# A forget gate's power by halves of the tokens, weight splits tied behind its series, and bias tiles by pair of heads, in a fused two-layer decoder kernel

## The chip, the cores and the metric

The kernel runs on one core of a Trainium2 chip. The metric is device time in microseconds (us) of one execution, and the median over several runs is compared. The engines are named as in the profile: PE is TensorE (matmuls and transposes), DVE is VectorE, ACT is ScalarE, POOL is GpSimd, and SP is SyncE, whose queue issues nearly all DMAs. Each engine works through its own queue of instructions in order and waits there for what an instruction needs.

## The reference

Two decoder layers work on 256 tokens of width 1024 in float32: a mixture of dilated sliding-window attentions with a SwiGLU feed-forward, then "forgetting attention" with another feed-forward. The change lies in the forgetting attention:

```
proj = h @ w_in
q, k, v = qkv[:, :, 0], qkv[:, :, 1], qkv[:, :, 2]
log_f = log_sigmoid(proj[..., 3 * ATTN_WIDTH:] + b_f)        # 16 heads, 256 tokens
c = cumsum(log_f, axis=1)
s = (q @ k^T) * scale + c[query] - c[key]                    # causal
o = softmax(s) @ v
```

The term c[query] is the same for a whole row of the softmax, so that only a bias by key, taken from c, has to be added to the scores before the mask and the softmax.

## The kernel before, in words

Matrix products are computed at nearly float32 accuracy from two halves. A weight piece of 128x2048 floats is loaded as two `raw` tiles of 128x1024 (SP, L89, five buffers). ACT casts each to `wh` (L74) and DVE writes the rest to `wl` = raw - wh (L76); `wh` and `wl` have four buffers each, one for each piece. `mm3` (L188) then makes three matmuls of each product: high by high, high by low, low by high. `weights` (L142) hands out a piece, and issues the load, the cast and the split of all pieces up to AHEAD = 2 further along a fixed order. In the forgetting layer this order is GATED (the values of heads 8 to 11 with the 16 gate columns), two pieces of values, and then, by quarter of the heads, (0,0), (0,1), (1,0), (1,1), (2,0), (2,1), (3,0), (3,1), (3,2): in (quarter, w), w = 0 is q, 1 is k and 2 is v. A quarter is four heads, and two pairs `pr` of heads.

The stage runs so. PE projects GATED for the first 128 tokens (t = 0), then the other two pieces of values for them, then the same for t = 1. After each GATED projection DVE adds the bias `bf` to the gate columns (L867) and so fills half of tile `gates` (128 tokens by 2 x 16). The second `norm_t` (L173) runs in the middle of the t = 0 values: DVE scales `xn` in two halves (L179) and PE transposes them (L184). After the second GATED projection `log1p` (L776) works on both halves at once, 128x32: two DVE instructions, a power e^t on POOL (L780), and 14 more DVE instructions, a series for log(1 + e^t). It has high priority in the scheduler, which decides the order on each engine when the kernel is built.

Then PE goes through the units: (0,0), (0,1), (1,0) and so on, each 48 matmuls of 256 columns, in two halves c of 24. `gates_2` (L791) is due after the first half of unit (0,0): two transposes of the gates on PE (L795), a cumulative sum on DVE (the scan of L799), and two DMAs that write it to tile `sums` in HBM (L801). `bias(hq)` (L803) reads the sums of four heads back, broadcast to all 128 partitions (L806, 128x1536, two buffers), and adds the causal mask to two blocks of each head on POOL (L808, 128x1024). It is due after unit (0,0) for quarters 0 and 1, and later for quarters 2 and 3.

`scores_b(hq, pr)` (L814) lets PE compute the scores of a pair into two PSUM banks `sc` (L822); DVE adds the bias (L828), which frees the bank, takes the row maximum (L832), ACT takes the exponential (L277), and DVE and ACT scale by the reciprocal sum (L839, L838). For quarter 0 the first pair's scores stand after the first half of unit (1,0) and the second pair's after its second half. Both use the same two `sc` banks: the second waits until the first pair's two bias adds have read them.

Of the kernel before, what the change touches and what calls it, by code (L numbers as in the profile page):

```python
# [10 lines left out]
F32 = mybir.dt.float32  # L11
F32R = mybir.dt.float32r
AF = mybir.ActivationFunctionType
ALU = mybir.AluOpType
AX = mybir.AxisListType

P = 128
# [3 lines left out]
NH = 16  # L21
# [10 lines left out]
def trunk(ctx: ExitStack, tc: tile.TileContext, T, out):  # L32
    nc = tc.nc
# [3 lines left out]
    ap = ctx.enter_context(tc.tile_pool(name="ap", bufs=1))  # L37
# [5 lines left out]
    def first():  # L43

        return tc.high_priority(offset=300)

    def psum(tag):
        return ps.tile([P, 512], F32, tag=tag, name=f"ps_{tag}", bufs=2)
# [10 lines left out]
    def const(name, shape):  # L59
        c = cst.tile(shape, F32, name=name)  # L60
        nc.sync.dma_start(c, T[name])
        return c
# [5 lines left out]
    euler = cst.tile([P, 1], F32, name="euler")  # L68
# [60 lines left out]
    order = [("a_in", hq * 9 + g * 3 + w) for hq, g, w in a_units]  # L129
# [8 lines left out]
    AHEAD = 2  # L138
    ready = {}
    state = {"next": 0}  # L140

    def weights(nm, i, after=None):  # L142

        upto = order.index((nm, i)) + AHEAD
        while state["next"] <= min(upto, len(order) - 1):
            key = order[state["next"]]
            cuts = []
            ready[key] = piece(key, cuts)
            for cut in cuts:
                cut(after)  # L150
            state["next"] += 1
        return ready.pop((nm, i))
# [147 lines left out]
    def stat_tile(tag, n):  # L300
        return ap.tile([P, n], F32, tag=tag, name=tag, bufs=3)
# [14 lines left out]
    for i, c in enumerate(room):  # L316
        b = 1 + (i > 1)
        n = S + 512
# [31 lines left out]
    sums = ap.tile([P, D], F32, tag="xn", name="sums", bufs=2)  # L350
# [3 lines left out]
    def square(i):  # L354
        return nc.scalar.activation(part[i].rearrange("p (j s) -> p j s", s=S), xs[i], AF.Square, scale=D ** -0.5)
# [5 lines left out]
    for k in range(KT):  # L361
        if k % 4 == 0:
            w = tuple(wp.tile([P, 2048], F32R, tag=y, name=y, bufs=4) for y in ("wh", "wl"))
        g, u = g_a[:, k:k + 1], slice(k % 4 * 512, k % 4 * 512 + 512)
        with first(), in_order(cut):
            if k == 0:
                a = nc.vector.tensor_scalar(hi[:, k], xk[k], g, None, op0=ALU.mult)
            else:
                a = nc.scalar.activation(hi[:, k], xk[k], AF.Copy, scale=g)
            b = nc.vector.scalar_tensor_tensor(lo[:, k], xk[k], g, hi[:, k].bitcast(F32), op0=ALU.mult,  # L370
                                               op1=ALU.subtract)
            with in_order((a, b)):
                cut = split(w, lambda y: y[:, u], wk[k])
        if k in (1, 5, 7):
            with first(), in_order(cut):
                a = [square(i) for i in {1: (0, 1), 5: (2,), 7: (3,)}[k]][-1]
# [12 lines left out]
    with first(), in_order(cut):  # L389
        a = square(4)  # L390
# [130 lines left out]
    def later(i, fn, *a):  # L521
        due.setdefault(i, []).append((fn, a))

    quads = [{"hq": hq, "fm": {}, "pt": {}, "v": {}} for hq in range(4)]
    for i, (hq, g, w) in enumerate(a_units):
        quad = quads[hq]
        if i == 3:
            o = o_next
        elif i:

            wt = weights("a_in", hq * 9 + g * 3 + w, read if i > 4 else None)
# [9 lines left out]
        if i in (24, 31):  # L541
            x.append(hrow("x"))
            t = len(x) - 1
            nc.sync.dma_start(x[t], T["x"][t * P:(t + 1) * P, :])
        if w < 2:
# [4 lines left out]
            if i == 2:  # L550
                values_12(quad["v"], lead)

                wt = weights("a_in", 1)
# [13 lines left out]
            if w == 1:  # L567

                j = i + (hq == 0)
# [5 lines left out]
                if g == 2:  # L575
                    later(j + 1, softmax_a, quad)
                    j = 9 * hq + 11 + 2 * (hq == 0)
# [8 lines left out]
        elif i > 1:  # L586


            half = hq % 2 if g == 0 else g - 1
# [164 lines left out]
    causal = const("causal", [P, P])  # L754
# [17 lines left out]
    ga = ap.tile([P, 6, 2 * NH], F32, tag="gates", name="gates", bufs=1)  # L772
    sums = dr.tile([NH, 3 * P], F32, name="sums")
    own = (slice(0, 64), slice(64, 128))

    def log1p():  # L776
        zt, m, t, s, w, a = (ga[:, i, :] for i in range(6))
        nc.vector.tensor_scalar(m, zt, -1.0, 0.0, op0=ALU.mult, op1=ALU.max)
        nc.vector.scalar_tensor_tensor(t, m, -2.0, zt, op0=ALU.mult, op1=ALU.subtract)
        nc.gpsimd.tensor_tensor(t, euler.to_broadcast([P, 2 * NH]), t, op=ALU.pow)  # L780
        nc.vector.tensor_scalar(s, t, 0.5, 1.0, op0=ALU.mult, op1=ALU.add)
        nc.vector.reciprocal(s, s)
        nc.vector.tensor_tensor(s, s, t, op=ALU.mult)
        nc.vector.scalar_tensor_tensor(w, s, 0.25, s, op0=ALU.mult, op1=ALU.mult)
        nc.vector.tensor_scalar(a, w, 1.0 / 17, None, op0=ALU.mult)
        for n in (15, 13, 11, 9, 7, 5, 3):
            nc.vector.scalar_tensor_tensor(a, a, 1.0 / n, w, op0=ALU.add, op1=ALU.mult)
        nc.vector.scalar_tensor_tensor(a, a, 1.0, s, op0=ALU.add, op1=ALU.mult)
        nc.vector.tensor_tensor(m, m, a, op=ALU.add)

    def gates_2():  # L791

# [7 lines left out]
        for y, n in ((0, P), (P, S)):  # L800
            nc.sync.dma_start(sums[:, y:y + n], cs[:, :n])  # L801

    def bias(hq):  # L803

        b = ap.tile([P, 12 * P], F32, tag="bias", name="bias", bufs=2)
        nc.sync.dma_start(b, sums[hq * 4:hq * 4 + 4].rearrange("h c -> (h c)").partition_broadcast(P))  # L806
        d = b.rearrange("p (h b j) -> p h b j", h=4, b=3)[:, :, 0:3:2]
        nc.gpsimd.tensor_tensor(d, d, causal[:, None, None, :].to_broadcast([P, 4, 2, P]), op=ALU.add)  # L808
        bq[hq]["bias"] = b

    ot = fm_tile("ot", KT, 1)
    bq = {hq: {} for hq in range(4)}

    def scores_b(hq, pr):  # L814
        b = bq[hq]
        nm = stat_tile("nm_b", 4)
        den = stat_tile("den_b", 4)
        pt = b.setdefault("pt", {})
        scs = [psum("sc") for _ in range(2)]
        for qb in range(2):  # L820
            for h in range(2):
                last = nc.tensor.matmul(scs[h][:, qb * P:qb * P + (qb + 1) * P], b[0][own[h], pr, qb * P:(qb + 1) * P],  # L822
                                        b[1][own[h], pr, :(qb + 1) * P], start=True, stop=True)
        for h in range(2):
            s = p_tile()
            with first():
                n = (pr * 2 + h) * 3 * P
                nc.vector.tensor_tensor(s[:, :3 * P], scs[h][:, :3 * P], b["bias"][:, n:n + 3 * P], op=ALU.add)  # L828
            for qb in range(2):
                j = h * 2 + qb  # L830
                sv = s[:, qb * P:qb * P + (qb + 1) * P]
                nc.vector.tensor_reduce(nm[:, j:j + 1], sv, axis=AX.X, op=ALU.max, negate=True)  # L832
                exps(sv, nm, den, j)
            pt[pr, h] = s
        c = stat_tile("c_b", 4)
        nc.vector.reciprocal(c, den)
        for h in range(2):
            nc.scalar.activation(pt[pr, h][:, :P], pt[pr, h][:, :P], AF.Copy, scale=c[:, h * 2:h * 2 + 1])  # L838
            nc.vector.tensor_scalar(pt[pr, h][:, P:3 * P], pt[pr, h][:, P:3 * P], c[:, h * 2 + 1:h * 2 + 2], None,  # L839
                                    op0=ALU.mult)  # L840
        return last
# [12 lines left out]
        split(ot, lambda x: x[:, hq * 2 + pr, :], o[:, :S])  # L854

    wz, oz = weights(*GATED), [psum("sc") for _ in range(2)]
    ws = [weights("b_in", i * 3 + 2) for i in range(2)]
    os = [psum("mm") for _ in range(2)]
    vs = [v_tile() for _ in range(3)]

# [10 lines left out]
        bq[i][2] = vs[i]  # L871
    for t in range(2):
        proj_gated(t)
        if t == 1:
            with first():
                log1p()
        for i in range(2):
            hook = (6, lambda: norm_t(*hs[1], g_b, xt, 1)) if i > t else None
            proj_pair(xt, ws[i], os, i, (t,), hook)
        v_pair(vs[:2], os[t], t)  # L880
    later(2.5, gates_2)
    for hq in range(2):
        later(3, bias, hq)
    for i, (hq, w) in enumerate(b_units):
        if i < 3:
            continue
        wt = weights("b_in", hq * 3 + w)
        o = psum("mm")
        if w < 2:
            for c in range(2):  # L890
                proj_feat(xt, wt, o[:, c * S:(c + 1) * S], c)
                if c == 0:
                    for fn, a in due.pop(i - 0.5, ()):
                        fn(*a)
            if w == 0:

                for fn, a in due.pop(i, ()):
                    fn(*a)
            bq[hq][w] = ap.tile([P, 2, S], F32, tag=f"fm{w}", name=f"fb{w}", bufs=2)
            nc.scalar.activation(bq[hq][w], o.rearrange("p (a b) -> p a b", a=2), AF.Copy, scale=(0.125, 1.0)[w])  # L900
            if w == 1:
                j = i + 1

                for pr in range(2):
                    due.setdefault(j - 0.5 + pr / 2, []).insert(0, (scores_b, (hq, pr)))
                if hq < 2:
                    later(j + 1, bias, hq + 2)
                later(j + 1, trans_b, hq, 0)
                later(j + 1.5, pv_b, hq, 0)
                later(j + 1.5, trans_b, hq, 1)  # L910
                later(j + 2, pv_b, hq, 1)
        else:
            for t in range(2):
                proj_tok(xt, wt, o[:, t * S:(t + 1) * S], t)
                if t == 0:
                    for fn, a in due.pop(i - 0.5, ()):
                        fn(*a)
            bq[hq][w] = v_tile(o)
        for fn, a in due.pop(i, ()):
            fn(*a)  # L920
# [20 lines left out]
    for o, (a, b) in zip(acc, ((0, 512), (512, 256), (768, 256))):  # L941
        s = slice(a, a + b)
# [109 lines left out]
```

## Time and profile before

| What | Value |
|---|---|
| time, median of 3 runs | 760.62 us (759.85 to 761.73) |
| the profiled execution's own time | 759.32 us |
| its span, first to last instruction | 757.5 us |
| PE busy | 743.0 us (98%) |
| DVE, ACT, POOL busy | 500.8, 374.8, 60.5 us |
| mean granted TensorE clock | 0.994 |
| moved by DMA | 138.08 MB, mean 182 GB/s |

The profile is of one execution. A timeline row gives the start in us, the duration, the engine, the line, the operation, output<-input, the number of instructions, and in brackets the idle time before it with what ended it; a row of several instructions gives their common stretch. A matmul's duration overlaps the next one's: what PE needs for one is read from the distance of the starts.

### The profile page before, as it was taken

What the parts mean: (1) busy time and instruction counts of PE and PEld (TensorE: products, weight loads), DVE (VectorE), ACT (ScalarE), POOL (GpSimd) and SP (SyncE); (2) the same over time, 40 slices, a digit from 0 to 9 for tenths busy, and PEclk for the clock granted to TensorE, in tenths of its full rate; (3) what the DMA queues carried; (4) which work ended last, traced back from release to release, by engine and by line L of the source; (5) the groups of instructions that cost most, each with busy time, mean ns of one, the idle gap of its engine ahead of it and who ended that gap; (6) DMA issues with size and microseconds to landing.
All of it is one profiled execution on the core that took longest, in us unless ns stands there. A gap on an engine that the chain in (4) does not pass through costs nothing.

```text
span 757.5 us, 14517 instructions
## 1 busy us (share of the span) xinstructions
PE 743.0 (98%) x6008; PEld 684.8 (90%) x6008; DVE 500.8 (66%) x756; ACT 374.8 (49%) x620; POOL 60.5 (8%) x93
## 2 busy tenths in 40 slices
PE   9999999999999999999999998899999999999996
PEld 7998989999988899999999987889889999999995
DVE  6997977876887566555555474599756655556533
ACT  7636347436346555344554444367645434455421
POOL 0600003004003000000000012221000000000000
PEclk9999999999999999999999999899999999999999
DMA  9955554553655266655667353854426665556601
GB/s 335 307 178 168 182 187 124 203 195 115 195 178 182 81 225 226 197 192 186 203 198 246 125 177 114 284 181 159 161 81 224 226 198 192 188 201 204 215 2 55
DMA packets 39010, 138.08 MB, mean 182 GB/s; under 512 B 4480, under 2 KB 5920, under 8 KB 38944
## 3 DMA queue, kind: packets, MB, share of 16 engines
q1 hardware_dynamic: 38800, 137.06, 54.4%
q8 instruction: 47, 0.77, 0.4%
q14 instruction: 19, 0.16, 0.1%
q10 hardware_dynamic: 144, 0.10, 0.0%
HBM read 136.07 MB, written 1.07 MB: 181 GB/s over the span
## 4 chain that ended last, share of the span: by engine, by line
PE 90%; issue 3%; ACT 2%; DVE 2%; DMA 2%; POOL 1%; SPq 0%; POOLq 0%; ACTq 0%; DVEq 0%
PE ps_mm L196 31%; PE ps_mm L191 16%; PE ps_tr L196 9%; PE ps_sc L196 8%; PE ps_o L196 7%; PE ps_tr L191 5%; PE ps_sc L191 4%; PE ps_o L191 3%; PE ps_o L298 2%; PE ps_tr L287 2%; ACT wh L74 1%; PE ps_sc L822 1%; PE ps_sc L444 1%; DMA otl<-in_lead 1%; PE ps_sc L460 1%
## 5 line engine op out<-in xcount | busy, mean ns | idle before, releaser
L74 ACT ACTIVATE wh<-raw 128x1024 fp32r<-128x1024 f32 x236 | 243.9, 1055 | 251.3 <-PE ps_mm L196 88.2
L76 DVE TENSOR_TENSOR wl<-raw,wh 128x1024 fp32r<-128x1024 f32 x236 | 287.7, 1238 | 90.1 <-ACT wh L74 89.9
L191 PE MATMUL ps_mm<-xt,wh 128*128 128x256 f32 x816 | 228.9, 281 | 0.5 <-DVE qk L428 0.5
L196 PE MATMUL ps_mm<-xt,wl 128*128 128x256 f32 x816 | 227.2, 279 | 0.1
L196 PE MATMUL ps_mm<-xt,wh 128*128 128x256 f32 x816 | 226.9, 278 | 0.0
L191 PEld LDWEIGHTS ps_mm<-xt,wh 128*128 128x128 f32 x816 | 154.6, 190 | 4.2 <-issue 3.3
L196 PEld LDWEIGHTS ps_mm<-xt,wl 128*128 128x128 f32 x816 | 154.5, 189 | 0.4 <-DVE wl L76 0.3
L196 PEld LDWEIGHTS ps_mm<-xt,wh 128*128 128x128 f32 x816 | 154.5, 189 | 0.0
L196 PE MATMUL ps_tr<-xt,wh 128*128 128x256 f32 x304 | 83.8, 276 | 0.0
L196 PE MATMUL ps_tr<-xt,wl 128*128 128x256 f32 x304 | 83.8, 276 | 0.0
L191 PE MATMUL ps_tr<-xt,wh 128*128 128x256 f32 x304 | 83.6, 276 | 0.0
L687 DVE TENSOR_TENSOR sa<-ps_tr,sa 128x256 f32<-128x256 f32 x38 | 16.1, 424 | 73.9 <-PE ps_tr L196 73.9
L196 PEld LDWEIGHTS ps_tr<-xt,wl 128*128 128x128 f32 x304 | 57.1, 188 | 0.0
L196 PEld LDWEIGHTS ps_tr<-xt,wh 128*128 128x128 f32 x304 | 57.0, 188 | 0.0
L191 PEld LDWEIGHTS ps_tr<-xt,wh 128*128 128x128 f32 x304 | 56.9, 188 | 0.0
L191 PE MATMUL ps_mm<-wh,xt 128*128 128x256 f32 (+1 forms) x160 | 53.0, 331 | 0.0
L196 PE MATMUL ps_mm<-wh,xt 128*128 128x256 f32 (+1 forms) x164 | 51.9, 320 | 0.0
L196 PE MATMUL ps_mm<-wl,xt 128*128 128x256 f32 (+1 forms) x164 | 51.8, 320 | 0.0
L273 POOL COPY v<-v 32x256 f32<-32x256 f32 x64 | 33.2, 519 | 179.6 <-ACT v L269 176.9
L161 POOL TENSOR_SCALAR rs<-ssq 128x1 f32<-128x1 f32 x7 | 2.2, 319 | 429.6 <-ACT junk L170 429.6
L196 PEld LDWEIGHTS ps_mm<-wl,xt 128*128 128x128 f32 x164 | 30.8, 188 | 2.5
L196 PEld LDWEIGHTS ps_mm<-wh,xt 128*128 128x128 f32 x164 | 30.5, 188 | 2.6
(218 smaller groups left out, 1136.9 us busy)
## 6 DMA issues: line engine op xcount, KB each, us to landing
raw<-in_gu SPq DMA_DIRECT2D x88, 512.0 KB, 4.4
raw<-in_a_in SPq DMA_DIRECT2D x68, 512.0 KB, 4.7
raw<-in_dn SPq DMA_DIRECT2D x44, 512.0 KB, 4.6
raw<-in_b_in SPq DMA_DIRECT2D x24, 512.0 KB, 4.6
raw<-in_a_out SPq DMA_DIRECT2D x8, 512.0 KB, 5.1
raw<-in_b_out SPq DMA_DIRECT2D x8, 512.0 KB, 4.4
bias<-sums SPq DMA_DIRECT2D x4, 768.0 KB, 5.1
grow<-in_norms SPq DMA_DIRECT2D x4, 512.0 KB, 5.8
```

The costliest lines, as they stand in the source:

```text
L74: a = nc.scalar.activation(view(hi), src, AF.Copy)
L76: return a, nc.vector.tensor_tensor(view(lo), src, view(hi).bitcast(F32), op=ALU.subtract)
L161: nc.gpsimd.tensor_scalar(m, s, rest, None, op0=ALU.add)
L191: nc.tensor.matmul(o, sh, mh, start=start, stop=False)
L196: last = nc.tensor.matmul(o[:, u], s, m[:, u], start=False, stop=end and u.stop == n)
L273: nc.gpsimd.tensor_copy(v[1 + a % 2][n:n + 32, a // 2 * S:a // 2 * S + S], by_t[a * 32:a * 32 + 32, t, g])
L287: nc.tensor.transpose(tr[:, i * P:(i + 1) * P], b, ident)
L298: nc.tensor.matmul(o[h * HD:(h + 1) * HD], v[:, c:c + HD], w(h), start=start, stop=stop)
L444: nc.tensor.matmul(scs[h][:, qb * P:qb * P + (qb + 1) * P], q[hr[h], pr, qb * P:(qb + 1) * P], k[hr[h], pr, :(qb + 1) * P], start=True, st ...
L460: nc.tensor.matmul(sc[h][c, o:o + 64], q[hr[h], pq, qb * P + a * 32:qb * P + a * 32 + 32], k[hr[h], pq].rearrange("p (b n) -> p b n", b=2) ...
L687: nc.vector.tensor_tensor(a, u, sg, op=ALU.mult)
L822: last = nc.tensor.matmul(scs[h][:, qb * P:qb * P + (qb + 1) * P], b[0][own[h], pr, qb * P:(qb + 1) * P], b[1][own[h], pr, :(qb + 1) * P], ...
```

## The change

- `power(half)` takes the two DVE instructions and POOL's power out of `log1p` and runs them on 128x16: for the tokens of t = 0 after their GATED projection, and for t = 1 after theirs, directly ahead of the rest of `log1p`, which stays on both halves.
- `weights` gets its reach as an argument. The second piece of values now reaches one piece ahead, not two, so that piece (0,1) is loaded and split with the unit (0,0), together with (1,0). These four splits on DVE are tied behind the last instruction of `log1p` (their ACT casts are not).
- `bias` works by pair of heads: DMAs of 128x768, masks of 128x512, and four buffers of half the size. Quarter 0's two are due after unit (0,0), as before, and quarter 1's two after unit (1,0).

Nothing of what is computed changes. The diff, cut to its core (`log1p`'s unchanged lines left out):

```
-    def weights(nm, i, after=None):
-        upto = order.index((nm, i)) + AHEAD
+    def weights(nm, i, after=None, ahead=AHEAD):
+        upto = order.index((nm, i)) + ahead
...
-    def log1p():
-        zt, m, t, s, w, a = (ga[:, i, :] for i in range(6))
+    def power(half):
+        zt, m, t = (ga[:, i, half * NH:(half + 1) * NH] for i in range(3))
         nc.vector.tensor_scalar(m, zt, -1.0, 0.0, op0=ALU.mult, op1=ALU.max)
         nc.vector.scalar_tensor_tensor(t, m, -2.0, zt, op0=ALU.mult, op1=ALU.subtract)
-        nc.gpsimd.tensor_tensor(t, euler.to_broadcast([P, 2 * NH]), t, op=ALU.pow)
+        nc.gpsimd.tensor_tensor(t, euler.to_broadcast([P, NH]), t, op=ALU.pow)
+
+    def log1p():
+        _, m, t, s, w, a = (ga[:, i, :] for i in range(6))
...
-        nc.vector.tensor_tensor(m, m, a, op=ALU.add)
+        return nc.vector.tensor_tensor(m, m, a, op=ALU.add)
...
-    def bias(hq):
-        b = ap.tile([P, 12 * P], F32, tag="bias", name="bias", bufs=2)
-        nc.sync.dma_start(b, sums[hq * 4:hq * 4 + 4].rearrange("h c -> (h c)").partition_broadcast(P))
-        d = b.rearrange("p (h b j) -> p h b j", h=4, b=3)[:, :, 0:3:2]
-        nc.gpsimd.tensor_tensor(d, d, causal[:, None, None, :].to_broadcast([P, 4, 2, P]), op=ALU.add)
-        bq[hq]["bias"] = b
+    def bias(hq, pr):
+        b = ap.tile([P, 6 * P], F32, tag="bias", name="bias", bufs=4)
+        nc.sync.dma_start(b, sums[hq * 4 + pr * 2:hq * 4 + pr * 2 + 2].rearrange("h c -> (h c)").partition_broadcast(P))
+        d = b.rearrange("p (h b j) -> p h b j", h=2, b=3)[:, :, 0:3:2]
+        nc.gpsimd.tensor_tensor(d, d, causal[:, None, None, :].to_broadcast([P, 2, 2, P]), op=ALU.add)
+        bq[hq]["bias", pr] = b
...
-    ws = [weights("b_in", i * 3 + 2) for i in range(2)]
+    ws = [weights("b_in", i * 3 + 2, ahead=2 - i) for i in range(2)]
...
         proj_gated(t)
-        if t == 1:
-            with first():
-                log1p()
+        with first():
+            power(t)
+            last = log1p() if t else None
...
     for hq in range(2):
-        later(3, bias, hq)
+        for pr in range(2):
+            later(3 + 2 * hq, bias, hq, pr)
...
-        wt = weights("b_in", hq * 3 + w)
+        wt = weights("b_in", hq * 3 + w, last if i == 3 else None)
```

DVE's queue from the end of the two instructions ahead of the second (before: the only) power. Before, splits of weights (L76) stand between the instructions of the series:

```order
L779 SCALAR_TENSOR_TENSOR gates<-gates 128x32
L781 TENSOR_SCALAR gates<-gates 128x32
L782 RECIPROCAL gates<-gates 128x32
L76 TENSOR_TENSOR wl<-raw,wh 128x1024
L783 TENSOR_TENSOR gates<-gates 128x32
L76 TENSOR_TENSOR wl<-raw,wh 128x1024
L784 SCALAR_TENSOR_TENSOR gates<-gates 128x32
L785 TENSOR_SCALAR gates<-gates 128x32
L76 TENSOR_TENSOR wl<-raw,wh 128x1024
L787 SCALAR_TENSOR_TENSOR gates<-gates 128x32
L76 TENSOR_TENSOR wl<-raw,wh 128x1024
L787 SCALAR_TENSOR_TENSOR gates<-gates 128x32 x5
```

The same place of the changed kernel, in whose numbering L784 to L792 are the series and L802 is the scan:

```order
L779 SCALAR_TENSOR_TENSOR gates<-gates 128x16
L784 TENSOR_SCALAR gates<-gates 128x32
L785 RECIPROCAL gates<-gates 128x32
L786 TENSOR_TENSOR gates<-gates 128x32
L787 SCALAR_TENSOR_TENSOR gates<-gates 128x32
L788 TENSOR_SCALAR gates<-gates 128x32
L790 SCALAR_TENSOR_TENSOR gates<-gates 128x32 x7
L791 SCALAR_TENSOR_TENSOR gates<-gates 128x32
L792 TENSOR_TENSOR gates<-gates 128x32
L76 TENSOR_TENSOR wl<-raw,wh 128x1024 x5
L802 SCALAR_TENSOR_TENSOR v<-v,ps_tr 16x256
L76 TENSOR_TENSOR wl<-raw,wh 128x1024 x5
```

The series now stands in one piece. Five splits have moved behind it and ahead of the scan, the sixth behind the scan.

SP's queue from the load of a norm's row (`grow`) on, while PE still projects the gates' second half; before:

```order
L56 DMA grow<-in_norms 128x1024
L89 DMA raw<-in_b_in 128x1024 x6
L801 DMA sums<-v 16x128
L801 DMA sums<-v 16x256
L89 DMA raw<-in_b_in 128x1024
L806 DMA bias<-sums 128x1536 x2
L89 DMA raw<-in_b_in 128x1024 x3
L806 DMA bias<-sums 128x1536
```

And in the changed kernel:

```order
L56 DMA grow<-in_norms 128x1024
L89 DMA raw<-in_b_in 128x1024 x4
L804 DMA sums<-v 16x128
L804 DMA sums<-v 16x256
L89 DMA raw<-in_b_in 128x1024 x2
L809 DMA bias<-sums 128x768 x4
L89 DMA raw<-in_b_in 128x1024 x2
L809 DMA bias<-sums 128x768
```

The sums are written after four loads of weights, not six, and the first read of the bias stands behind six such loads, not seven. On PE the two transposes of the gates stand behind 24 matmuls of unit (0,0), where they stood behind 38; from the first scores on, PE's order is the same.

More of the change, by code (lines that the diff above doesn't have):

```diff
@@ L826, in scores_b @@
             with first():
-                n = (pr * 2 + h) * 3 * P
-                nc.vector.tensor_tensor(s[:, :3 * P], scs[h][:, :3 * P], b["bias"][:, n:n + 3 * P], op=ALU.add)
+                bias_h = b["bias", pr][:, h * 3 * P:(h + 1) * 3 * P]
+                nc.vector.tensor_tensor(s[:, :3 * P], scs[h][:, :3 * P], bias_h, op=ALU.add)
             for qb in range(2):
@@ L906, in trunk @@
                 if hq < 2:
-                    later(j + 1, bias, hq + 2)
+                    for pr in range(2):
+                        later(j + 1, bias, hq + 2, pr)
                 later(j + 1, trans_b, hq, 0)
```

## The prediction

> **What bounds the kernel now.** I read the page first: how busy PE is says whether other engines matter at all. Its rows are the share of the span, and the granted clock in 40 slices.
>
> ```profile
> span 757.5 us, 14517 instructions
> PE 743.0 (98%) x6008; PEld 684.8 (90%) x6008; DVE 500.8 (66%) x756; ACT 374.8 (49%) x620; POOL 60.5 (8%) x93
> PEclk9999999999999999999999999899999999999999
> ```
>
> PE sets the end. A change can only gain where PE stands still or runs slowly, and the one slice with an 8 lies at 473 to 492 us. So the waits of PE come next (us in total, times, longest):
>
> ```profile
> PE ps_tr L795 <- DVE gates L789: 5.7, 1, 5.7
> PE ps_o L307 <- POOL euler L69: 0.9, 1, 0.9
> PE ps_mm L191 <- DVE qk L428: 0.5, 1, 0.5
> ```
>
> One wait is worth having: the transposes of the gates for the series. PE's timeline around it, and the windows after it (length, PE busy, clock, DMA share, GB/s):
>
> ```profile
> 466.43 0.29 PE L191 MATMUL ps_mm<-xt,wh 128*128 128x256 f32 x1
> ...
> 470.63 0.28 PE L196 MATMUL ps_mm<-xt,wh 128*128 128x256 f32 x1
> 476.61 0.60 PE L795 MATMUL ps_tr<-ident,gates 128*16 128x128 f32 x2 [5.70 <-DVE gates L789]
> 476.86 0.56 PE L196 MATMUL ps_mm<-xt,wl 128*128 128x256 f32 x1
> 477.22 0.42 PE L191 MATMUL ps_mm<-xt,wh 128*128 128x256 f32 x1
> ...
> 482.30 0.28 PE L191 MATMUL ps_mm<-xt,wh 128*128 128x256 f32 x1
> ...
> 488.65 0.28 PE L196 MATMUL ps_mm<-xt,wl 128*128 128x256 f32 x1
> 488.86 0.93 PE L822 MATMUL ps_sc<-fb,fb 64*128 64x128 f32 x8
> ...
> 492.65 1.03 PE L822 MATMUL ps_sc<-fb,fb 64*128 64x128 f32 x8
> 476.60:482.30 5.70, 5.69 (x28) 0.51 0.67 236
> 482.30:488.65 6.35, 6.35 (x58) 1.00 0.93 308
> ```
>
> From 482.30 to 488.65 there are 56 steps of 0.1134 us each. From 477.22 to 482.30 there are 24 matmuls at 0.212: after the wait PE runs for 5.7 us at clock 0.51. That is a second price of the same wait: 24 x (0.212 - 0.1134) = 2.4, and about 0.3 for the transposes and the matmul behind them. The wait costs 5.7 + 2.4 + 0.3 = 8.4 us. Another way gives the same: unit (0,0) starts at 466.43, and 120 matmuls stand before the first scores (38 ahead of the transposes, 82 behind them); 120 x 0.1134 = 13.6, with 0.4 for the transposes 480.4, against 488.86.
>
> The Trainium skill (TensorE: Matmul & The Clock Gate, Part 1) says that an idle window of about 3.4 us halves the clock and about 3.4 us of work restores it. The halving agrees; the slow stretch here was 5.7 us, so the measured price of 2.7 stands, where 3.4 us at half speed would be an estimated 1.7.
>
> Why DVE is late, from its own timeline and POOL's:
>
> ```profile
> 461.11 0.17 DVE L867 TENSOR_TENSOR gates<-ps_sc,bf 128x16 f32<-128x16 f32 x1 [2.67 <-PE ps_sc L196]
> 461.54 0.19 DVE L779 SCALAR_TENSOR_TENSOR gates<-gates 128x32 f32<-128x32 f32 x1
> 467.27 0.18 DVE L781 TENSOR_SCALAR gates<-gates 128x32 f32<-128x32 f32 x1 [5.54 <-POOL gates L780]
> 467.49 0.35 DVE L782 RECIPROCAL gates<-gates 128x32 f32<-128x32 f32 x1
> 472.76 1.09 DVE L787 SCALAR_TENSOR_TENSOR gates<-gates 128x32 f32<-128x32 f32 x5
> 475.01 1.22 DVE L76 TENSOR_TENSOR wl<-raw,wh 128x1024 fp32r<-128x1024 f32 x1
> 476.14 0.18 DVE L788 SCALAR_TENSOR_TENSOR gates<-gates 128x32 f32<-128x32 f32 x1
> 477.24 0.68 DVE L799 TENSOR_TENSOR_SCAN v<-v,ps_tr 16x256 f32<-16x256 f32 x1 [0.69 <-PE ps_tr L795]
> 452.37 1.56 POOL L164 TENSOR_TENSOR rs<-rs,mhalf 128x1 f32<-128x1 f32 x1 [0.33 <-DVE gates L867]
> 461.81 5.43 POOL L780 TENSOR_TENSOR gates<-euler,gates 128x32 f32<-128x32 f32 x1 [7.89 <-DVE gates L779]
> L164 POOL TENSOR_TENSOR rs<-rs,mhalf x7: 566/572/1557, 255.2 to 747.0; 128x1 f32<-128x1 f32 x7
> ```
>
> The power holds the series until 467.27; then six splits share DVE with it until 476.55.
>
> **The change part by part.** *Power by halves.* The 128x32 power took 5.43 us, a 128x1 power 0.57. The line through both gives 0.57 + 15 x 0.157 = 2.9 for 128x16; the ends are 2.7 (half) and 5.43 (nothing saved). I take 2.9. The first half's power starts about 454.9 and is over by 457.8, or a microsecond later if it is stretched as the power at 452.37 was beside a split; nothing on POOL stands behind it. It costs DVE two instructions of 0.2 us, one between the two halves of `xn`: the second half ends 0.2 later, hidden by PE's first four transposes; uncovered, 0.2 us. The second power starts at 461.85 as before and ends at 464.75.
>
> *The series in one piece.* 14 instructions, 13 at 0.22 (five took 1.09) and the reciprocal at 0.38: 3.2 us, from 464.8 to 468.0. PE comes to the transposes after 24 matmuls, at 466.43 + 24 x 0.1134 = 469.15. That is 1.1 us of cover: the wait of 5.7 and the slow clock go, 8.4 us. With a power of 5.43 the series would end at 470.5 and PE wait 1.4.
>
> *The splits behind it.* Each takes 1.13 (475.01 to 476.14). Unit (0,1) starts at 466.43 + 48 x 0.1134 + 0.4 = 472.3 and needs its two, done at 469.1 and 470.3; unit (1,0), at 477.7, has its own by 472.5. No wait, with 2 us of cover; uncovered, the lateness itself. ACT's casts keep their order. Its copy of unit (0,0)'s result must free a PSUM bank by 477.7; it stands behind a cast whose load is issued at 470.3 and lands, at a median of 5.2 us, at 475.5, so the copy ends at about 477.1: covered by 0.6.
>
> ```profile
> DMA to landing us min/median/max: 4.0/5.2/6.0
> 468.95 7.63 SPq L89 DMA_DIRECT2D raw<-in_b_in  x6
> 477.94 0.81 SPq L801 DMA_DIRECT2D sums<-v  x2
> 482.00 0.85 SPq L806 DMA_DIRECT2D bias<-sums  x2
> DMA to landing us min/median/max: 3.4/3.5/3.6
> DMA to landing us min/median/max: 4.1/6.0/7.5
> 488.16 5.86 POOL L808 TENSOR_TENSOR bias<-bias,causal 128x1024 f32<-128x1024 f32 x2 [20.92 <-DMA bias<-sums]
> 499.04 2.40 POOL L808 TENSOR_TENSOR bias<-bias,causal 128x1024 f32<-128x1024 f32 x1 [5.02 <-DMA bias<-sums]
> 491.70 1.01 DVE L828 TENSOR_TENSOR p<-ps_sc,bias 128x384 f32<-128x384 f32 x2
> 488.66 3.12 DVE L76 TENSOR_TENSOR wl<-raw,wh 128x1024 fp32r<-128x1024 f32 x1 [0.20 <-ACT wh L74]
> ```
>
> The three lines of landings are those of the six weight loads of 465 to 480, of the two writes of the sums, and of the first three bias reads.
>
> *The bias by pairs.* This is what can come late next. Before, the first pair's adds ended at 492.71 and PE began the second pair's scores, which overwrite their banks, at 492.65: no slack. PE now comes there 3.8 us (492.65 - 488.86) after 480.4, at 484.2. The bias: five splits (5.65) stand ahead of the scan, which ends at 468.0 + 5.65 + 0.7 = 474.4; the second write is issued at 474.8 and lands after 3.5, at 478.3. The sixth load ahead of the bias needs the sixth split, over at 475.5, and holds nothing up. So the first read goes at 478.3, 3.7 earlier than before. Its landing: the first 768 KB read took 6.0, a lone one 4.1; for 384 KB behind two weight loads I take 4.0, with 3.0 and 6.0 as ends: 482.3. The mask of half the size: half of 2.40 to half of 3.4 (488.16 to about 491.6, when the first add waited for it), 1.4 taken, 2.4 if halving saves nothing: 483.7. Two adds, 1.0: 484.7. PE waits 0.5 us. By the ends: 0, or 478.3 + 6.0 + 2.4 + 1.0 - 484.2 = 3.5.
>
> A rule that speaks against halving the reads, from the Trainium skill (DMA: Bandwidth & Descriptors, Anatomy of one DMA): about 2.0 us of each DMA is fixed, the rest goes by 436 GB/s. The lone read agrees roughly (estimate 3.8, measured 4.1); for 384 KB it gives an estimate of 2.9, and PE would not wait: 752.2.
>
> Eight masks of half the size instead of four: the POOL work is the same. While a mask ran, a split took 3.12 instead of 1.22; that happens in shorter pieces, and PE waited for none of it before. A quarter-2 read now stands in SP's queue ahead of loads for units 30 us away: nothing.
>
> **Sum.** -8.4 + 0.5 = -7.9. The profiled execution, 759.32, would take 751.4; the median, 760.62, lies 1.3 above it and becomes **752.7**. A difference under 0.3% (2.3 us) can't be told from none here.
>
> **The rivals.** *The bias later still (0.18).* Longer reads or masks, up to the ends above: PE waits 1.5 to 3.5, giving 753.7 to 755.7; if the clock falls after such a wait as it did after 5.7, another 2.7, up to 758.4. For it: adds and scores met without slack before. Against it: the reads are half as long.
>
> *The power doesn't shrink (0.06).* PE waits 1.4 at the transposes; all behind the series comes 2.55 later, so the adds end at 487.25 against 485.6: 3.1 lost, 755.3. Against: the 0.57 of one column.
>
> *The first power holds DVE (0.03).* If POOL's power comes ahead of the second half of `xn` on what they share, as the mask did to the split, that half waits up to 2.9, PE up to 2.5: 8.4 - 0.5 - 2.5 gives 755.2. Against: `xn` starts as L779 ends, the power some 0.1 later.
>
> *The wait only moves (0.04).* If reads and masks saved nothing at all, the adds would follow the scan's end by 492.71 - 477.92 = 14.8, at 489.2: a wait of 5.0 and 2.7 of slow clock against the 8.4, 759.9: no change.
>
> *Slower (0.03).* If something pins the adds to the clock time they have now (the sums' write or the reads held by the weight loads, which are all issued earlier), PE comes at 484.2 and waits until 492.7: 8.5 + 2.7 - 8.4 = 2.8 slower, 763.4. It is slower by over 0.3% only if the adds end after 492.2. Against: the only loads ahead of the reads are free by 475.5.
>
> **How the numbers follow.** The forecast has 0.66. Its wait of 0 to 1.5 gives 752.2 to 753.7; the runs shown scatter by 0.9 around their median, so I start at 751.0. Rivals two and three and most of the first lie under 756.0, which is the upper end. Faster: 0.66 + 0.18 + 0.06 + 0.03, less 0.02 for the first rival's far end: 0.91. Same: 0.04 + 0.02 = 0.06. Slower: 0.03.
>
> **What would show it.** Right: no wait of PE at the gates' transposes, clock 1.00 from 475 to 485, a power of about 2.9 us, series over at 468, first scores at about 480.4, first mask starting near 482.3. Wrong: a wait of PE at the second pair's scores of over 1.5 us, or of any length at the transposes; a power near 5 us; a slow clock after either.

## The result, and the profile after

The changed kernel took **754.2 us** in the median of five runs (753.28 to 755.8), the kernel before, on the same chip, 760.63. The ratio is 0.9915, with a 95% interval of 0.9899 to 0.9931: faster by 6.4 us, inside the range, 1.5 us above the number forecast. Below, differences of under 0.3% are again told as none, unless their interval is narrower.

The page of the changed kernel, its span, its busiest engine and the granted clock in 40 slices. The profiled execution is the slowest of the five, 755.8 us:

```profile
span 754.0 us, 14536 instructions
PE 742.7 (98%) x6008; PEld 683.7 (91%) x6008; DVE 499.1 (66%) x758; ACT 376.2 (50%) x620; POOL 61.9 (8%) x98
PEclk9999999999999999999999999999999999999999
```

The slice with an 8 is gone. The waits of PE (us in total, times, longest):

```profile
PE ps_sc L825 <- DVE p L831: 2.0, 1, 2.0
PE ps_sc L380 <- ACT wh L74: 1.0, 2, 0.8
PE ps_o L307 <- POOL euler L69: 0.9, 1, 0.9
```

The 5.7 us at the gate transposes are gone too, and the series' last instruction is in no row. A new wait stands first: the second pair's scores (L825) wait for the adds of the bias (L831). The two others lie in the first 60 us of the kernel. PE's timeline through the stage, in this execution, whose unit (0,0) begins 0.5 us later than in the one of before (466.95 against 466.43):

```profile
469.69 0.38 PE L798 MATMUL ps_tr<-ident,gates 128*16 128x128 f32 x2
481.08 0.93 PE L825 MATMUL ps_sc<-fb,fb 64*128 64x128 f32 x8
486.90 1.38 PE L825 MATMUL ps_sc<-fb,fb 64*128 64x128 f32 x8 [1.97 <-DVE p L831]
```

The transposes come without a wait, and the first scores 7.8 us earlier than at 488.86. From there to the second scores it took 3.8 us before; now it is 5.8, because of the 1.97 in brackets. The windows behind the transposes and behind that wait (length, PE busy, clock, DMA share, GB/s):

```profile
476.60:484.70 8.10, 8.10 (x71) 1.00 0.99 310
486.90:492.00 5.10, 5.10 (x27) 0.67 0.92 305
```

Where PE ran at 0.51 before, it now runs at 1.00. But behind the new wait the clock fell in this execution: 5.1 us at 0.67, that is 5.1 x (1 - 0.67) = 1.7 us lost. Next, POOL's and DVE's timelines, for the power and the series:

```profile
455.39 3.35 POOL L780 TENSOR_TENSOR gates<-euler,gates 128x16 f32<-128x16 f32 x1 [0.95 <-DVE gates L779]
462.31 2.90 POOL L780 TENSOR_TENSOR gates<-euler,gates 128x16 f32<-128x16 f32 x1 [3.57 <-DVE gates L779]
465.25 0.18 DVE L784 TENSOR_SCALAR gates<-gates 128x32 f32<-128x32 f32 x1 [3.02 <-POOL gates L780]
468.34 0.19 DVE L792 TENSOR_TENSOR gates<-gates 128x32 f32<-128x32 f32 x1
468.45 5.76 DVE L76 TENSOR_TENSOR wl<-raw,wh 128x1024 fp32r<-128x1024 f32 x5
474.13 0.67 DVE L802 TENSOR_TENSOR_SCAN v<-v,ps_tr 16x256 f32<-16x256 f32 x1
```

A power of 2.90, a series of 3.28 in one piece (465.25 to 468.53), five splits in 5.76, and the scan over at 474.80. The way from there to the adds, by SP's issues, POOL's masks and DVE's adds:

```profile
469.70 3.73 SPq L89 DMA_DIRECT2D raw<-in_b_in  x4
474.82 0.81 SPq L804 DMA_DIRECT2D sums<-v  x2
475.74 0.84 SPq L89 DMA_DIRECT2D raw<-in_b_in  x2
479.47 2.91 SPq L809 DMA_DIRECT2D bias<-sums  x4
484.99 4.96 POOL L811 TENSOR_TENSOR bias<-bias,causal 128x512 f32<-128x512 f32 x4 [19.77 <-DMA bias<-sums]
486.29 1.02 DVE L831 TENSOR_TENSOR p<-ps_sc,bias 128x384 f32<-128x384 f32 x2 [3.46 <-POOL bias L811]
```

And the landings behind the two writes of the sums, and behind the four reads:

```profile
DMA to landing us min/median/max: 4.2/4.3/4.4
DMA to landing us min/median/max: 5.4/6.2/6.9
```

The scan is 3.1 us earlier than before, the first read 2.5 (479.47 against 482.00), the first mask 3.2 (484.99 against 488.16). PE, however, came to its second scores 7.7 us earlier. Ahead of the reads six loads of weights are issued within ten microseconds; four of them had landed by 479.0, and two were still in flight when the first read went out (issued at 475.7 and 476.2, landed at 480.3 and 481.6). The write took 4.2 to 4.4 where 3.5 was taken, the first read 5.4 where 4.0 was.

### The profile page after: what moved, and what is told of

Read it like the earlier page. It is cut to its first block, busy times and chain, and to the rows that moved or that the text cites. A ratio compares the mean times of both kernels' runs of the same rounds, so it can differ in the third digit from the quotient of the medians.

```text
span 754.0 us, 14536 instructions
## 1 busy us (share of the span) xinstructions
PE 742.7 (98%) x6008; PEld 683.7 (91%) x6008; DVE 499.1 (66%) x758; ACT 376.2 (50%) x620; POOL 61.9 (8%) x98
## 4 chain that ended last, share of the span: by engine, by line
PE 90%; DMA 2%; issue 2%; ACT 2%; DVE 2%; POOL 1%; SPq 0%; POOLq 0%; DVEq 0%; ACTq 0%
PE ps_mm L196 31%; PE ps_mm L191 16%; PE ps_tr L196 9%; PE ps_sc L196 8%; PE ps_o L196 7%; PE ps_tr L191 5%; PE ps_sc L191 4%; PE ps_o L191 3%; PE ps_o L298 2%; PE ps_tr L287 2%; DMA otl<-in_lead 1%; ACT wh L74 1%; PE ps_sc L444 1%; PE ps_sc L825 1%; PE ps_sc L460 1%
## 5 line engine op out<-in xcount | busy, mean ns | idle before, releaser
L76 DVE TENSOR_TENSOR wl<-raw,wh 128x1024 fp32r<-128x1024 f32 x236 | 286.1, 1233 | 85.0 <-ACT wh L74 84.9
L191 PE MATMUL ps_mm<-xt,wh 128*128 128x256 f32 x816 | 228.7, 281 | 0.0
L191 PEld LDWEIGHTS ps_mm<-xt,wh 128*128 128x128 f32 x816 | 154.2, 189 | 3.7 <-issue 3.3
L191 PE MATMUL ps_tr<-xt,wh 128*128 128x256 f32 x304 | 83.6, 276 | 0.0
L191 PEld LDWEIGHTS ps_tr<-xt,wh 128*128 128x128 f32 x304 | 56.9, 188 | 0.0
L191 PE MATMUL ps_mm<-wh,xt 128*128 128x256 f32 (+1 forms) x160 | 53.0, 331 | 0.0
```

What stands on the lines that cost most here:

```text
L76: return a, nc.vector.tensor_tensor(view(lo), src, view(hi).bitcast(F32), op=ALU.subtract)
L191: nc.tensor.matmul(o, sh, mh, start=start, stop=False)
```

## The experiments

Each is set against runs of the kernel before on the same chip. The question is what the three parts are worth, and why the read of the bias is late.

### The bias by quarters again (e1)

The changed kernel with the third part undone:

```
-    def bias(hq, pr):
-        b = ap.tile([P, 6 * P], F32, tag="bias", name="bias", bufs=4)
+    def bias(hq):
+        b = ap.tile([P, 12 * P], F32, tag="bias", name="bias", bufs=2)
...
-        for pr in range(2):
-            later(3 + 2 * hq, bias, hq, pr)
+        later(3, bias, hq)
```

> The change with the bias by quarters again (768 KB reads, 128x1024 masks), power by halves and tied splits kept. Theory A (the changed kernel stands still at the second pair's scores because the bias reads queue behind weight loads on the DMA engines, and the pairs make read and mask shorter): the first read lands about 1 us later than the pair's 5.4, the mask takes 2.4 to 3.4 instead of 1.3, so the adds come 2 to 3 us later and PE waits 4 to 5 us there, with a slow clock behind it: 757.5 to 760. Theory B (a read back of the sums takes over 5 us whatever its size and whatever is queued): only the mask is longer, PE waits about 3.1: 755 to 757.

Measured: 758.68 us against 760.05, ratio 0.9979 (0.9969 to 0.9988). PE's second scores and POOL's masks, on their timelines:

```profile
489.93 2.11 PE L825 MATMUL ps_sc<-fb,fb 64*128 64x128 f32 x8 [3.85 <-DVE p L831]
486.94 4.65 POOL L811 TENSOR_TENSOR bias<-bias,causal 128x1024 f32<-128x1024 f32 x2 [20.67 <-DMA bias<-sums]
```

The window behind those scores (columns as above):

```profile
489.90:496.40 6.50, 6.47 (x30) 0.52 0.64 243
```

A wait of 3.85, and then 6.5 us at 0.52, which cost 3.1: most of the 8.4 us saved at the transposes is given back at the next wait. With the other two parts in place the pairs are worth 4 to 5 us (a gain of 1.4 by quarters, of 6.4 and, in another batch, 5.5 by pairs, each against the kernel before on its own chip), although no engine does less work for it.

### The bias by pairs alone (e2)

The kernel before with that third part only:

```
-        later(3, bias, hq)
+        for pr in range(2):
+            later(3 + 2 * hq, bias, hq, pr)
```

> The kernel before with only the third part of the change: the bias tiles and their mask by pair of heads; the power stays whole (128 x 32) and the weight splits keep their place. Theory A (what remains to be gained lies behind the log1p, and the pairs matter only once the tensor engine no longer waits at the gate transposes): the wait of 5.7 us at the transposes and the slow clock behind it stay, and since that wait holds the second pair's scores back as well, the bias is there in time by quarters as by pairs: the same time as before, 759 to 761 us, within 0.3%. Rival theory P (the bias by pairs has a worth of its own, whatever the tensor engine waits for ahead of it): 1 to 3 us faster, 757 to 759.

Measured: 760.1 against 760.48, ratio 0.9995 (0.9985 to 1.0004). PE's wait:

```profile
PE ps_tr L795 <- DVE gates L789: 5.7, 1, 5.7
```

DVE's first adds and PE's second scores, on their timelines:

```profile
491.97 0.93 PE L822 MATMUL ps_sc<-fb,fb 64*128 64x128 f32 x8
489.92 1.01 DVE L828 TENSOR_TENSOR p<-ps_sc,bias 128x384 f32<-128x384 f32 x2
```

The wait stands as it was. The adds come 1.8 us earlier than before (491.70), PE's scores 0.7 (492.65), so that 1.0 us of slack has come between them; it is worth nothing, because before the adds had ended just as PE came. So the same edit is worth nothing here and 4 to 5 us behind the other two. Theory A holds.

### The power by halves alone (e3)

The kernel before with the first part only; the weight splits stay between the instructions of the series:

```
-        if t == 1:
-            with first():
-                log1p()
+        with first():
+            power(t)
+            last = log1p() if t else None
```

> The kernel before with the power by halves alone. The power ends 2.5 us earlier, the six splits still stand between the instructions of the series, the transposes still behind 38 matmuls: PE's wait there falls from 5.7 to about 3.2. If the clock falls behind it as before: 758.1; if it doesn't: 755.4. If the splits and not the power set the end of the series, the wait stays near 5.7 and the time at 760.6.

Measured: 757.59 against 760.05, ratio 0.9963 (0.995 to 0.9975). PE at the transposes:

```profile
474.85 0.60 PE L798 MATMUL ps_tr<-ident,gates 128*16 128x128 f32 x2 [3.14 <-DVE gates L792]
```

And the window from there on:

```profile
474.80:480.00 5.20, 5.15 (x35) 0.74 0.67 236
```

The wait falls from 5.7 to 3.14, by the 2.5 that the power is shorter; the rest stays with the splits, and with it a slow clock, milder than before (0.74 over 5.2 us). Another 1.2 us are waited at the second scores.

### The tie alone (e4)

The kernel before with the second part only: the power stays 128x32.

```
-    ws = [weights("b_in", i * 3 + 2) for i in range(2)]
+    ws = [weights("b_in", i * 3 + 2, ahead=2 - i) for i in range(2)]
...
-        wt = weights("b_in", hq * 3 + w)
+        wt = weights("b_in", hq * 3 + w, last if i == 3 else None)
```

> The kernel before with the splits tied behind the series alone (one 128x32 power, bias by quarters). The power ends at 467.3, the series in one piece 3.2 later at 470.5, the transposes stand behind 24 matmuls at 469.2: a wait of 1.4 there. Everything behind comes 2.5 us later than in the run with power by halves, tie and quarters, which waited 3.85 for the bias: here 4.9, with the slow clock behind it: 760 to 762, no gain.

Measured: 759.25 against 759.5, ratio 0.9999 (0.9987 to 1.001). PE's three waits of the stage:

```profile
PE ps_sc L825 <- DVE p L831: 4.6, 1, 4.6
PE ps_tr L798 <- DVE gates L792: 1.3, 1, 1.3
PE ps_mm L191 <- ACT fb L904: 0.8, 1, 0.8
```

1.3 at the transposes, as the sum said of a power that doesn't shrink (1.4), but then 4.6 at the second scores (4.9 was expected) and a slow clock behind it, 2.1 us lost. The tie alone moves the wait and gains nothing; the 0.8 at L191 is the bank that the prediction covered by 0.6.

### The reads ahead of two loads (e5)

Now the read itself. In the changed kernel the fifth and sixth loads stand ahead of the reads, and more behind the first reads. Here two loads wait in SP's order for the first read:

```
+            held = (key, c) in ((("b_in", 2 * 3 + 1), 1), (("b_in", 3 * 3), 0))
+            with tc.issue_after(bq[0]["read"].ins) if held else nullcontext():
+                nc.sync.dma_start(raw, T[key[0]][key[1]][:, u])
```

> The changed kernel with the two weight loads that SP issued between the write of the sums and the first bias read now issued behind the four bias reads. Theory A: the first read lands in 3 to 4 us instead of 5.4, the wait of 2.0 at the second pair's scores falls to 0.3 or less: 752.2 to 752.6. Theory B: the landing stays over 5 and the wait at 1.6 to 2: 754.0 give or take 0.4.

Measured: 757.12 against 760.05, ratio 0.9964 (0.9952 to 0.9977). That is a gain of 2.9 us where the changed kernel gained 6.4 and, in another batch, 5.5; its intervals, up to 0.9931 and 0.9945, don't meet this one. The reads' issue, the first mask, and ACT's cast of a displaced load:

```profile
479.87 1.78 SPq L811 DMA_DIRECT2D bias<-sums  x4
483.77 4.99 POOL L813 TENSOR_TENSOR bias<-bias,causal 128x512 f32<-128x512 f32 x4 [18.56 <-DMA bias<-sums]
487.88 1.06 ACT L74 ACTIVATE wh<-raw 128x1024 fp32r<-128x1024 f32 x1 [6.80 <-DMA raw<-in_b_in]
```

All four loads ahead of it have landed, by 479.4, when the first read is issued. It lands after 3.8 us instead of 5.4, and the wait at the second scores falls to 0.7. But the cast at 487.88 waits 6.8 us for its load and stands ahead of the exponentials on ACT, and of the 1.28 us in which ACT loads its table of functions (L279): PE waits 1.6 us at the scores of the pair after and 0.7 at two transposes. The read came earlier as theory A said, though not to the 0.3 us of wait; the cure cost more than it saved. Of this kernel's time 2.4 us lie in none of these waits. For 0.9 of them the reason is that its profiled execution is, at 756.27, faster than the median; for the rest I haven't found where.

### The scan behind two splits, not five (e7)

The splits of piece (1,0), which PE needs last, are tied behind the scan. Later loads wait for the `raw` buffers that these splits free, so that four loads, not six, stand ahead of the reads in SP's order:

```
+            if hold is not None and key != (nm, i + 1):
+                hold.extend(cuts)
+                cuts = []
...
+        for cut in hold:
+            cut(scan)
```

> The changed kernel with only two weight splits, not five, between the series and the scan on DVE; piece (1,0)'s two are tied behind the scan. Both theories: the scan ends about 3.4 us earlier (near 471.4 instead of 474.8), the adds come before PE needs the banks, no wait at the second pair's scores: about 752.2. If the time stays near 754.2, the wait there is not what the forecast missed by.

Measured: 754.92 against 760.05, ratio 0.9931 (0.9919 to 0.9943). No wait at the second scores any more; ACT's cast and PE's new waits, by their timelines:

```profile
486.71 1.06 ACT L74 ACTIVATE wh<-raw 128x1024 fp32r<-128x1024 f32 x1 [5.55 <-DMA raw<-in_b_in]
492.72 0.95 PE L290 MATMUL ps_tr<-ident,p 128*128 128x128 f32 x6 [1.01 <-ACT p L846]
497.73 0.93 PE L830 MATMUL ps_sc<-fb,fb 64*128 64x128 f32 x8 [1.32 <-ACT fb L910]
```

The 752.2 expected was missed, for the same reason as in the kernel ahead of it: a cast whose load now comes late stands on ACT ahead of the exponentials. The mechanism on DVE was right (the scan ends at 471.82), the queue on ACT was left out of the sum. Here that is read from the timelines; the next kernel moves the cast.

### The scan early, and that cast behind the exponentials (e8 and e10)

The kernel ahead, with this one cast tied behind the first pair's last exponential:

```
+            for c, cut in enumerate(cuts):
+                with tc.issue_after(bq[0]["exp"].ins) if (key, c) == (("b_in", 2 * 3 + 1), 1) else nullcontext():
+                    cut(after)
```

> The early scan again, with the cast of piece (2,1)'s second half tied behind the last exponential of the first pair on ACT. Theory A (every wait left of PE in this stage comes from the bias chain or from ACT standing before that cast, whose load was pushed behind the reads): PE waits nowhere from the gates to the second quarter's scores by more than 0.3 us, and the 8.4 us of the old wait are gained in full: 8.4 under the kernel before, about 751.7 where that takes 760.1. Theory C (some other limit, DMA or DVE, takes the gain back): waits of 1 us and more remain at the transposes of the probabilities, time within 1 us of the changed kernel's.

And for the second time that it ran, in another batch:

> The kernel of e8 once more, beside the two others on the same chip, so that the bias by quarters can be set against it there. Expected: e8's 751.8 us within 0.3%, and no wait of the tensor engine between the gate transposes and the second pair's scores.

Measured: **751.82** against 759.5, ratio 0.9897 (0.9879 to 0.9916); again, in another batch, **752.25** against 760.48, ratio 0.9892 (0.9878 to 0.9905). The first execution's timelines of SP, POOL, DVE and PE:

```profile
476.27 1.75 SPq L815 DMA_DIRECT2D bias<-sums  x4
480.16 1.28 POOL L817 TENSOR_TENSOR bias<-bias,causal 128x512 f32<-128x512 f32 x1 [15.12 <-DMA bias<-sums]
482.44 1.01 DVE L837 TENSOR_TENSOR p<-ps_sc,bias 128x384 f32<-128x384 f32 x2
484.68 0.93 PE L831 MATMUL ps_sc<-fb,fb 64*128 64x128 f32 x8
```

And PE's window over the whole stage:

```profile
470.00:495.00 25.00, 25.00 (x217) 1.00 0.88 311
```

PE runs through from 470 to 495 at full clock. The adds are over 1.2 us ahead of the second scores. That is nearly the whole gain forecast for the transposes: 8.4 us, measured 7.7 and 8.2. And with the cast moved the two waits of the kernel ahead are gone. It beats the kernel before and the changed one, the latter by 2.2 us as it ran in the same batch (754.05, ratio 0.9931, 0.9917 to 0.9945: the two intervals lie side by side).

### The same with the bias by quarters (e12)

```
-        for pr in range(2):
-            later(3 + 2 * hq, bias, hq, pr)
+        later(3, bias, hq)
```

> The fastest version so far (e8: scan behind two splits, the cast of the late load behind the first pair's exponentials) with the bias by quarters of the heads again in place of pairs. In e8 the read of a pair landed 3.8 us after issue, its mask took 1.28, and the first pair's adds ended at 483.45, 1.2 us ahead of the tensor engine's second scores at 484.68. By quarters a 768 KB read lands later (6.4 in e1 against 5.4 in the changed kernel, so at least 1.0 later) and its mask takes 1.0 to 1.1 longer. Theory A (the pairs matter by what they leave between the adds and the second scores): adds 2.1 to 3.7 later, a wait of 0.9 to 2.5 us at the second scores, 0.9 to 2.5 us above e8 and up to 2 more where the clock falls after it: 752.7 to 756. Rival theory P0 (with the scan early, the pairs are no longer needed): no wait there, and e8's time within 0.3%.

Measured: 753.53 against 760.48, ratio 0.9903 (0.9888 to 0.9918), 1.3 us above the kernel by pairs in the same batch (752.25). POOL's masks and PE's second scores:

```profile
483.98 4.69 POOL L817 TENSOR_TENSOR bias<-bias,causal 128x1024 f32<-128x1024 f32 x2 [18.40 <-DMA bias<-sums]
486.99 1.38 PE L831 MATMUL ps_sc<-fb,fb 64*128 64x128 f32 x8 [1.44 <-DVE p L837]
```

The wait of 1.44 is the difference. The two medians lie 0.17% apart, and their intervals against the kernel before overlap; it is the wait in the trace that bears theory A out.

### The reads from another queue (e9)

If SP's order alone held the reads, POOL could issue them itself:

```
-        nc.sync.dma_start(b, sums[...].rearrange("h c -> (h c)").partition_broadcast(P))
+        nc.gpsimd.dma_start(b, sums[...].rearrange("h c -> (h c)").partition_broadcast(P))
```

> The changed kernel with the bias reads issued from POOL's queue, so that SP's loads no longer stand behind them and SP never waits for the write of the sums. Theory A (the read is late because of what is queued on the shared DMA engines, not because of SP's order): loads go out earlier, nothing is moved from in front of the reads, the first read lands no earlier than in the changed kernel, PE waits 2 us or more at the second pair's scores: same time or up to 2 us slower than the changed kernel. Theory D (SP's queue holds the reads): the wait falls under 1, time 1 to 2 us under the changed kernel.

Measured: 758.69 against 759.5, ratio 0.9992 (0.9983 to 1.0001). POOL's timeline:

```profile
479.30 1.88 POOL L809 DMA_DIRECT2D bias<-sums  x3 [15.28 <-DMA sums<-v]
485.93 1.26 POOL L811 TENSOR_TENSOR bias<-bias,causal 128x512 f32<-128x512 f32 x1 [4.76 <-DMA bias<-sums]
```

The first mask starts 6.6 us after the first issue, 5.5 in the changed kernel: the read is slower from a queue of its own, and PE's wait grows to 3.93. SP, which no longer waits for the sums, had three loads in flight when the first read was issued and sent a fourth 0.1 us behind it. So SP's order is not what makes the read late. Whether these loads or the issue from POOL made it slower still, this run doesn't separate.

### The changed kernel again (e11)

No edit; it stands beside the early scan in one batch.

> The changed kernel itself once more, on the same chip as the others of this call: 0.9915 of the kernel before as in the first measurement, with a wait of about 2 us at the second pair's scores.

Measured: 754.05 against 759.5, ratio 0.9931 (0.9917 to 0.9945). PE at the second scores:

```profile
486.62 1.38 PE L825 MATMUL ps_sc<-fb,fb 64*128 64x128 f32 x8 [2.27 <-DVE p L831]
```

The window behind:

```profile
486.60:492.00 5.40, 5.38 (x42) 1.00 0.85 332
```

The wait is there again, longer by 0.3, but this time the clock stays at 1.00. So the 1.7 us of slow clock belong to one execution, not to the change; the last section shows on what it hung.

### The account

All kernels by the same sum. The waits are those of PE between 465 and 515 us, in one profiled execution of each; the slow clock is the length of the window behind a wait times one minus its granted clock; the last column is the median of before in the batch less the kernel's own, but for the changed kernel's profiled execution, which is set against that of before (759.32 - 755.8).

| kernel | waits, us | slow clock, us | 8.4 less both | measured gain |
|---|---|---|---|---|
| pairs alone | 5.7 | 2.4 | 0.3 | 0.4 |
| tie alone | 1.3 + 0.8 + 4.6 | 2.1 | -0.4 | 0.3 |
| power alone | 3.1 + 1.2 | 1.4 | 2.7 | 2.5 |
| quarters again | 3.9 | 3.1 | 1.4 | 1.4 |
| reads issued by POOL | 3.9 + 0.3 | 3.1 | 1.1 | 0.8 |
| reads ahead of two loads | 3.1 | 0 | 5.3 | 2.9 |
| changed, its profiled execution alone | 2.0 | 1.7 | 4.7 | 3.5 |
| changed, again | 2.3 + 0.4 | 0 | 5.7 | 5.5 |
| scan early | 1.3 + 1.0 | 0 | 6.1 | 5.1 |
| scan early, cast later, quarters | 1.4 | 0 | 7.0 | 7.0 |
| scan early, cast later | 0, 0.3 | 0 | 8.4, 8.1 | 7.7, 8.2 |

One stage accounts for nearly everything. The kernel with the reads ahead of two loads is off by 2.4, as told above; the changed kernel's one execution is off by 1.2, of which 0.5 is its late start.

## Why the prediction was right, and where it was off

The gain and its cause came as forecast; one of its own signs of being wrong came too, a wait of over 1.5 us at the second pair's scores. The time lies inside the range because the range took in most of the rival with that wait.

- **The price of the old wait, 8.4 us: right.** The kernel in which no wait stands in its place gained 7.7 and 8.2. The slow clock behind the wait was part of that price; counted by PE's waits alone it would have been 5.7.
- **The power at 2.9: right,** 2.90, by the line through the two widths that before showed. The first half's power took 3.35 beside the halves of `xn`, as allowed for, and nobody waited for it.
- **The series at 3.2 and the cover of 1.1 at the transposes: right.** 3.28, and no wait. Without the shorter power 1.3 was measured where 1.4 was worked out.
- **ACT's copy, covered by 0.6: held in one execution of two.** No wait in the first profile, 0.43 in the second, 0.77 with the tie alone. The 5.2 us taken for the landing of the load ahead of it were too few: that load took 5.6 and 6.2.
- **The wait at the second scores, 0.5: this step failed.** It was 1.97 and 2.27. Two terms of it were too small: the landing of the sums' write (3.5 taken, 4.2 to 4.4 measured, 4.7 to 4.9 in the second execution) and that of the first read (4.0 taken, 5.4 and 5.9). The first mask, forecast near 482.3, began at 484.99. The scan (474.4 forecast, 474.80 in an execution 0.5 later) and the mask (1.4 taken, 1.29 for the later mask that ran alone, at 492.27) were right. The write's 0.8 and the read's 1.4 came on top, 0.1 came off for the mask, and 0.4 for the adds: PE began its scores at 486.90, behind the first of the two adds, where the sum waited for both (they end at 487.31). That makes 1.7; 1.5 was missing at the scores (2.0 - 0.5), and the 754.2 lies 1.5 above the 752.7. So it was the first rival, the bias later still, that came, with a wait of its lower half. The forecast's own limit for that wait, 1.5, was too narrow.
- **Why the read was late: open.** The forecast took it to stand behind two loads, and two it was: the others had landed. So the term failed in its size, and no count of loads gives that size. Reads of 384 KB issued with two loads in flight took 5.4 and 5.9 in the changed kernel, but 4.2, 3.8 and 4.0 in the three executions with the early scan; with none in flight 3.8, with one 4.8 (pairs alone), with three, from POOL's queue, 6.6. What goes with the size is how much DMA had moved in the 4 us ahead of the issue: 350 to 389 GB/s ahead of the three that took 5.4 and more, 192 to 303 ahead of the five that took 4.8 and less. No run changes that rate alone, and the first reads of 768 KB, 6.0 to 6.9, don't follow it, so it isn't shown as the cause. By the Trainium skill (DMA: Bandwidth & Descriptors, Anatomy of one DMA) 384 KB would land in an estimated 2.9. That section gives its sum for DMAs issued by GpSimd, while these reads are SP's; no first read here was as fast, from either queue. Why the sums' write took 4.2 to 4.4, and with the reads ahead of two loads 4.6 to 4.8, stays open too.
- **The other rivals fell.** The power shrank, the first power held nobody, nothing pinned the adds. *The wait only moves* fell for the change as a whole, but is what the tie alone does (0.3 us, which is none).
- **The parts are not a sum.** Alone the power gained 2.5, the tie 0.3 and the pairs 0.4, the last two no more than none; together they gained 6.4. Each uncovers the wait that the next takes away: first at the series, then at the bias, which is late behind the scan.

```profile
492.27 1.29 POOL L811 TENSOR_TENSOR bias<-bias,causal 128x512 f32<-128x512 f32 x1 [2.32 <-DMA bias<-sums]
```

That is the mask that ran alone, on POOL's timeline of the changed kernel.

## What to carry to other kernels

When PE is pulled forward by some microseconds, list everything that it will meet in the next 20 us and work out when each is ready; the wait comes back at the first that isn't. A DMA on that path is costed neither by its size nor by the number of loads ahead of it: here the same read behind two loads took 3.8 to 5.9 us. If its bounds are wider than the slack behind it, the wait belongs in the forecast. And before a load is moved back to let such a DMA pass, look where its cast stands on ACT: in order behind it may be the very work that PE waits for, and the cast has to move too.

## What was unexpected of the hardware

- Whether the clock falls behind a wait of about 2 us depends on where the wait lies. Wherever it fell in this stage, it was 0.50, for 3.41 or 6.83 us; the 0.67 above is the mean of a longer window. Cut each trace into steps of 3.41 us, counted from a change of its own clock (in the second execution of the changed kernel, where none lies in this stage, from the fall at 748.87). In the seven traces in which the clock fell, PE was idle for 1.79 us or more of the step ahead of the fall; behind every step at full clock with 1.69 or less it stayed. The wait of 1.97 put 1.79 into one step, that of 2.27 was split into 1.69 and 0.58. Here are the steps of the changed kernel's first execution, then those of its second (length, PE busy, clock, DMA share, GB/s):

```profile
485.11:488.52 3.41, 1.62 (x10) 1.00 1.01 402
488.52:491.94 3.42, 3.42 (x18) 0.50 0.87 253
482.63:486.04 3.41, 1.72 (x15) 1.00 0.99 325
486.04:489.45 3.41, 2.83 (x20) 1.00 0.83 326
```

The steps lie differently in each execution, so the same wait can cost 1.7 us more or nothing. The Trainium skill (TensorE: Matmul & The Clock Gate, Part 1) puts the idle window at about 3.4 us. The length of the steps agrees; here a step idle for little over half was enough.
- Issuing a DMA takes longer on POOL, and counts there as work of the engine. On SP's queue the four reads of the early scan took 1.75 us, 0.44 each; on POOL three took 1.88, 0.63 each, while nothing else ran there.
